# A scheduler that keeps ScalarE's table, with begin times and first clock slices from the trace: a two-layer decoder trunk on one core

## The chip, the core and the metric

The kernel runs on one core of a Trainium2 chip. The metric is device time in microseconds: the median of three runs of the program. The engines are named as in the profile: PE (TensorE, with PEld for its weight loads), ACT (ScalarE), DVE (VectorE), POOL (GpSimd) and SP (SyncE, which here issues every DMA).

## The reference, cut to what matters

Two groups of tokens, 512 of a prompt and 8 x 8 of samples, go through two layers that share their weights. Layer 0 mixes by trailing means (windows 2, 4, 8 and 16) and a 256 x 256 map per group; layer 1 is a gated DeltaNet mixer with 16 value heads; a SwiGLU feed-forward net (FFN) follows each mixer, and RMS norms stand around everything.

```python
for i in range(DEPTH):                      # 2
    h = rms_norm(x, norm_mix_pre[i])
    if i % 2 == 0:
        m, nb = pool_mixer(h, ...)
    else:
        m, nc, ns = gdn_mixer(h, ...)       # projections, conv, gates, chunked delta rule, gate by silu(z), w_out
    x = x + rms_norm(m, norm_mix_post[i])
    h = rms_norm(x, norm_ffn_pre[i])
    x = x + rms_norm(swiglu(h, ffn_w_in[i], ffn_w_out[i]), norm_ffn_post[i])
```

All is float32. The large products are made of three float32r products of split operands (high x high, low x high, high x low).

## The kernel before, in words

Activations lie with channels on the partitions and the 576 tokens on the free axis, cut in two halves (256 + 320 or 288 + 288). Weights stream from HBM as 512 KB blocks: `wraw` is what a DMA brings, `wh` its rounded high part, made on ACT, and `wl` the rest, made on DVE; PE takes `wh` and `wl` as weights and `hH`, `hL` (or `aH`, `aL`; `dH`, `dL` in layer 0) as the other operand.

No engine's order is written by hand. Between `plan.start()` and `plan.finish()` each call is only recorded, by class `Plan`, with the tiles it reads and writes. `finish` then plays the program through a cost table (`cost`, `forward`): at each step the engine that is free first takes an instruction, by rank (the latest start that `backward` found). `take` chooses among those that are ready. A change of ScalarE's function table is priced at 1283 ns (`TURN`), and `HOLD` says by how many ns of rank an engine may pass over the best instruction for one that needs no change of mode. `refined` repeats this with pushed ranks; the pushes are drawn from seeds, and `CHOSEN` lists the seeds to be used, by stretch of the plan.

`forward` also keeps a model of PE's clock. `phases` holds four windows of 3413 ns that are a quarter apart; a window in which PE did less than the share `LOAD` of work makes PE half as fast in the next, and `fast` is the mean over the four (1.0 is full speed, 2.0 half). Where PE would stand idle for more than 300 ns, `idle_until` puts in fillers: products of `ones` with itself into a free PSUM bank, `ps_w`, that no one reads. One planned filler, a 128 x 128 float32 product, shows as two matmuls in the profile. `LEAVE` and `KEEP` limit them.

The names that the later sections use. At the start: `xt` are tiles of 128 prompt tokens; PE turns them (`ps_A<-ident,xt`), ACT sums their squares and makes the root `xst`, DVE takes the reciprocal and makes the normed `xn`, which PE multiplies by the window masks `bf`, `bm`, `bh`; the results go on as `dH`, `dL`. In the mixer of layer 1, `gates()` makes the decays: `misc` on ACT and DVE, the sum over time on PE (`ps_g<-t_le,misc`), a copy `gcr` that goes to HBM (`gc_d`), and a tile `gts` on DVE that uses the buffer of `gcr` again. `project` is the stream of `ps_m` products of the next head group, which fills PE. `gate()` ends a head: PE turns the head's output `vt` into PSUM (`ps_x<-ident,vt`), a DMA then brings `z` into the place of `vt`, and DVE multiplies the two. Ring `x` has one PSUM bank, so the next head's turn waits for that DVE instruction; below, the time from one turn to the next is called a round. There are four head groups of four heads; in the first three `z` comes by that DMA.

Line 478 is the recording layer's replay, so nearly every row has that line, and the fillers have line 474.

Of the kernel before, what the change touches and what calls it, by code (L numbers as in the profile page):

```python
# [57 lines left out]
class Plan:  # L58
# [15 lines left out]
    HOLD = {"PE": 2500.0, "ACT": 0.0}  # L74
    WINDOW, LOAD = 3413.0, 0.38
# [492 lines left out]
    def forward(self, rank, state=None, until=None):  # L568
# [4 lines left out]
        if state is None:  # L573
            todo = n
            left = [len(o[4]) for o in ops]
            free = dict.fromkeys(self.ENGINES, 0.0)
# [5 lines left out]
            phases = [[self.WINDOW * i / 4, 0.0, 2.0, 0, self.WINDOW * (4 - i) / 4] for i in range(4)]  # L582
            fast = 2.0
# [6 lines left out]
        else:  # L590
# [9 lines left out]
            phases = [p[:] for p in phases]  # L600
# [1584 lines left out]
```

## Time and profile before

| | before |
|---|---|
| time, median of 3 runs | 1514.92 us (1513.43 to 1515.28) |
| time of the profiled execution | 1514.92 us |
| its span | 1513.2 us |
| mean granted TensorE clock | 0.995 |
| PE, PEld busy | 1492.4 us (99%), 1445.6 us (96%) |
| DVE busy | 1130.1 us (75%) |
| ACT busy | 852.2 us (56%) |
| POOL busy | 112.1 us (7%) |
| HBM read, written | 165.60 MB, 30.52 MB |

The profiled execution took 1.72 us more than its span from the first to the last instruction, and its time is the median itself. A matmul's end is modelled and overlaps the next one's start, so the share of PE says that PE seldom stood still, not that it ran at its peak; the waits of PE and the places of the fillers tell more.

### The profile page before, as it was taken

Reading aid. Unit: us, or ns where it says so; the run is one execution under the profiler, and the core shown is the slowest. Engines: PE = TensorE matmul, PEld = TensorE weight load, DVE = VectorE, ACT = ScalarE, POOL = GpSimd, SP = SyncE. Lnnn points to the kernel's source line nnn. Section 1 sums busy time; section 2 is a strip of 40 time slices with the busy share of each in tenths; the row PEclk is TensorE's granted clock in tenths of the full one; section 3 lists DMA queues with packets and bytes.
Section 4 is the critical chain, followed back from the end, with each engine's and each line's share of the span. In section 5 each row is a group of like instructions: output and inputs, shape, how many; then the busy total and the mean of one; then the engine's idle time right before and its main releaser. Section 6 shows DMA issues by size and latency. Waiting matters only on the chain.

```text
span 1513.2 us, 30277 instructions
## 1 busy us (share of the span) xinstructions
PE 1492.4 (99%) x11790; PEld 1445.6 (96%) x11790; DVE 1130.1 (75%) x2280; ACT 852.2 (56%) x1839; POOL 112.1 (7%) x246
## 2 busy tenths in 40 slices
PE   8999999999999999999999999999999999999998
PEld 7999999999999899899899899899999999999997
DVE  6994566668789697996898798657796575756856
ACT  7763543435456865865684794645575453434545
POOL 4210000000001010110121110000110000000000
PEclk9999999999999999999999999999999999999999
DMA  7564233233467343434443534657864432324264
GB/s 191 146 184 127 83 88 92 80 102 111 125 181 194 90 126 111 125 99 125 130 113 94 147 113 127 199 157 215 248 193 145 127 97 86 93 81 121 65 163 136
DMA packets 344854, 197.86 MB, mean 131 GB/s; under 512 B 13499, under 2 KB 337692, under 8 KB 344703
## 3 DMA queue, kind: packets, MB, share of 16 engines
q1 hardware_dynamic: 344711, 195.92, 44.9%
q8 instruction: 93, 1.52, 0.4%
q14 instruction: 50, 0.41, 0.1%
HBM read 165.60 MB, written 30.52 MB: 130 GB/s over the span
## 4 chain that ended last, share of the span: by engine, by line
PE 57%; DVE 4%; ACT 2%; DMA 2%; issue 1%; SPq 0%; ACTq 0%; DVEq 0%
PE ps_m L478 16%; PE ps_A L478 15%; PE ps_B L478 14%; PE ps_s L478 5%; PE ps_k L478 4%; PE ps_x L478 2%; DVE vt L478 1%; DVE ac L478 1%; PE ps_n L478 1%; DMA vt<-z_d 1%; DVE wl L478 1%; DVE ii L478 0%; DMA out_dram<-St 0%; ACT wh L478 0%; DMA og<-og_d 0%
## 5 line engine op out<-in xcount | busy, mean ns | idle before, releaser
L478 ACT ACTIVATE wh<-wraw 128x1024 fp32r<-128x1024 f32 (+4 forms) x239 | 233.3, 979 | 202.6 <-PE ps_B L478 87.2
L478 DVE TENSOR_TENSOR wl<-wraw,wh 128x1024 fp32r<-128x1024 f32 (+4 forms) x238 | 266.2, 1123 | 82.8 <-ACT wh L478 48.1
L478 PE MATMUL ps_m<-hH,wh 128*128 128x320 f32 (+1 forms) x832 | 246.9, 311 | 0.3 <-ACT zz L478 0.3
L478 PE MATMUL ps_m<-hL,wh 128*128 128x320 f32 (+1 forms) x832 | 245.6, 307 | 0.0
L478 PE MATMUL ps_m<-hH,wl 128*128 128x320 f32 (+1 forms) x832 | 244.7, 307 | 0.0
L478 PEld LDWEIGHTS ps_m<-hH,wh 128*128 128x128 f32 x832 | 153.7, 189 | 4.3 <-issue 1.5
L478 PEld LDWEIGHTS ps_m<-hH,wl 128*128 128x128 f32 x832 | 154.1, 189 | 2.6 <-issue 1.3
L478 PEld LDWEIGHTS ps_m<-hL,wh 128*128 128x128 f32 x832 | 154.4, 189 | 1.9 <-issue 0.6
L478 PE MATMUL ps_B<-hH,wl 128*128 128x320 f32 (+1 forms) x444 | 128.7, 304 | 0.0
L478 PE MATMUL ps_B<-hL,wh 128*128 128x320 f32 (+1 forms) x444 | 128.4, 303 | 0.0
L478 PE MATMUL ps_B<-hH,wh 128*128 128x320 f32 (+1 forms) x444 | 128.0, 304 | 0.0
L478 PE MATMUL ps_A<-hH,wl 128*128 128x256 f32 (+1 forms) x432 | 118.9, 291 | 0.0
L478 PE MATMUL ps_A<-hH,wh 128*128 128x256 f32 (+1 forms) x432 | 118.8, 290 | 0.0
L478 PE MATMUL ps_A<-hL,wh 128*128 128x256 f32 (+1 forms) x432 | 118.4, 289 | 0.0
L478 PE MATMUL ps_A<-aL,wh 128*128 128x288 f32 (+2 forms) x408 | 113.8, 296 | 0.0
L478 PE MATMUL ps_A<-aH,wl 128*128 128x288 f32 (+2 forms) x408 | 113.4, 296 | 0.0
L478 PE MATMUL ps_A<-aH,wh 128*128 128x288 f32 (+2 forms) x408 | 113.2, 296 | 0.0
L478 PE MATMUL ps_B<-aH,wl 128*128 128x288 f32 x296 | 83.7, 297 | 0.1
L478 PE MATMUL ps_B<-aH,wh 128*128 128x288 f32 x296 | 83.0, 296 | 0.1
L478 PE MATMUL ps_B<-aL,wh 128*128 128x288 f32 x296 | 83.1, 295 | 0.0
L478 PEld LDWEIGHTS ps_B<-hH,wh 128*128 128x128 f32 x444 | 81.8, 188 | 0.3
L478 PEld LDWEIGHTS ps_B<-hH,wl 128*128 128x128 f32 x444 | 81.8, 188 | 0.1
(458 smaller groups left out, 3976.9 us busy)
## 6 DMA issues: line engine op xcount, KB each, us to landing
wraw<-in_ffn_w_in_dram SPq DMA_DIRECT2D x77, 512.0 KB
wraw<-in_gdn_w_in_dram SPq DMA_DIRECT2D x56, 512.0 KB
graw<-in_ffn_w_in_dram SPq DMA_DIRECT2D x33, 512.0 KB
wraw<-in_ffn_w_out_dram SPq DMA_DIRECT2D x32, 448.0 KB
wraw<-in_gdn_w_out_dram SPq DMA_DIRECT2D x24, 512.0 KB
wraw<-in_ffn_w_out_dram SPq DMA_DIRECT2D x32, 320.0 KB
St<-in_state_gdn_rec_dram SPq DMA_DIRECT2D x32, 256.0 KB
out_dram<-St SPq DMA_DIRECT2D x32, 256.0 KB
```

The source lines that it names most:

```text
L478: calls[e](*a, **k)
```

## The change

The diff, without the long table of seeds:

```diff
-    HOLD = {"PE": 2500.0, "ACT": 0.0}
-    WINDOW, LOAD = 3413.0, 0.38
+    HOLD = {"PE": 2500.0, "ACT": 1500.0}
+    WINDOW, LOAD = 3413.0, 0.40
+    BEGIN = {"PE": 0.0, "ACT": 2250.0, "DVE": 2250.0, "POOL": 2200.0, "SP": 150.0}
+    FIRST = 4250.0
...
     CHOSEN = (
-        "0: 7936 55843 86527 33991 97722 31117 8629 9687 47150 83676 16297 15132 53952 77128 31040 66847 59628 "
...
-            free = dict.fromkeys(self.ENGINES, 0.0)
+            free = dict(self.BEGIN)
...
-            phases = [[self.WINDOW * i / 4, 0.0, 2.0, 0, self.WINDOW * (4 - i) / 4] for i in range(4)]
-            fast = 2.0
+            phases = [[0.0, 0.0, 1.0, 0, self.FIRST + self.WINDOW * (1.0 + i / 4)] for i in range(4)]
+            fast = 1.0
```

ACT may now pass over an instruction for up to 1500 ns of rank rather than change its table. The engines' first planned instructions start at `BEGIN` and not all at zero. The modelled clock begins at full speed and stays there until the first windows end, 7663 to 10222 ns after the plan's zero, where before it began at half. `CHOSEN` has 2633 seeds in five strings in place of 2377 in four. No instruction computes anything else: the products are the same, and only the order, the engine of a few instructions that may run on either DVE or POOL, the fillers (31 in place of 21) and the table loads (27 in place of 26) differ. The orders of all engines differ in detail nearly everywhere. The source lines move by 18: 478 is now 496, and 474 is 492.

The first place is PE at the very start: fillers, the turning of the first `xt` tiles, and the first product with `xn`. Before:

```order
L474 MATMUL ps_w<-ones 128x128 x6
L478 MATMUL ps_A<-ident,xt 128x128 x12
L478 MATMUL ps_A<-bf_143,xn 128x128
L478 MATMUL ps_A<-ident,xt 128x128 x4
L478 MATMUL ps_n_169<-ident,prow 128x73
L478 MATMUL ps_A<-bf_143,xn 128x128
```

And now:

```order
L492 MATMUL ps_w<-ones 128x128 x13
L496 MATMUL ps_A<-ident,xt 128x128 x8
L492 MATMUL ps_w<-ones 128x128 x4
L496 MATMUL ps_A<-ident,xt 128x128 x8
L496 MATMUL ps_A<-bf_143,xn 128x128
L492 MATMUL ps_w<-ones 128x128
L496 MATMUL ps_A<-bf_143,xn 128x128
```

Thirteen fillers stand ahead of the first turn of `xt` where six stood, and four more inside the sixteen turns.

The second place is ACT in `gates()`, from the logarithm (`misc`) on; `bet` is the sigmoid, `qks` and `ac` are silus, `gce` is an exponential. Before:

```order
L478 ACT_TABLE_LOAD
L478 ACTIVATE misc<-misc 128x80
L478 ACTIVATE u,ksq<-ps_x 128x128 x3
L478 ACTIVATE u<-ps_m 128x256
L478 ACTIVATE u<-ps_m 128x8x8
L478 ACTIVATE u<-ps_e 128x256
L478 ACTIVATE ac<-u,cwt 128x600
L478 ACT_TABLE_LOAD
L478 ACTIVATE bet<-misc 128x80
L478 ACTIVATE gcr<-ps_g 16x512
```

And now:

```order
L496 ACT_TABLE_LOAD
L496 ACTIVATE misc<-misc 128x80
L496 ACTIVATE ac<-u,cwt 128x600
L496 ACT_TABLE_LOAD
L496 ACTIVATE qks<-ac 128x64
L496 ACTIVATE gcr<-ps_g 16x512
L496 ACTIVATE u<-ps_e 128x256
L496 ACTIVATE wh<-wraw 128x1024
```

One table load stands between the logarithm and `gcr` in both; it was the sigmoid's and is now the silu's, and the sigmoid comes later.

The third place is PE in the second head group, where the first group's heads are turned (`ps_x<-ident,vt`) between products of the projection; shown is the end of the first round, up to the second head's turn. Before:

```order
L478 MATMUL ps_k<-T_1791,Uw 64x32 x32
L478 MATMUL ps_m<-hH,wl 128x320
L478 MATMUL ps_m<-hH,wh 128x320
L478 MATMUL ps_m<-hL,wh 128x320
L478 MATMUL ps_m<-hH,wl 128x320
L478 MATMUL ps_m<-hH,wh 128x320
L478 MATMUL ps_m<-hL,wh 128x320
L478 MATMUL ps_m<-hH,wl 128x320
L478 MATMUL ps_m<-hH,wh 128x320
```

And now the whole round, from the first head's turn to the second's:

```order
L496 MATMUL ps_x<-ident,vt 128x128 x4
L496 MATMUL ps_m<-hH,wl 128x320
L496 MATMUL ps_m<-hH,wh 128x320
L496 MATMUL ps_m<-hL,wh 128x320
L496 MATMUL ps_m<-hH,wl 128x320
L496 MATMUL ps_m<-hH,wh 128x320
L496 MATMUL ps_k<-T_1791,Uw 64x32 x32
L496 MATMUL ps_m<-hL,wh 128x320
L496 MATMUL ps_m<-hH,wl 128x320
L496 MATMUL ps_m<-hH,wh 128x320
L496 MATMUL ps_m<-hL,wh 128x320
L496 MATMUL ps_x<-ident,vt 128x128 x4
```

The first round held eight products of 320 columns and six of 256 (two ahead of the rows shown, four behind them) and now holds nine of 320; the small products `T,Uw` are in both.

309 rows, old and new, of the table CHOSEN are left out of this document.

## The prediction

> **What bounds the kernel now.** I read the page first, then the waits of PE, then the timelines at the places where PE has fillers or waits. The first row is section 1 of the page (busy us, share, count), the second the row of ScalarE's table loads among the groups of instructions (busy us, mean ns, idle before).
>
> ```profile
> PE 1492.4 (99%) x11790; PEld 1445.6 (96%) x11790; DVE 1130.1 (75%) x2280; ACT 852.2 (56%) x1839; POOL 112.1 (7%) x246
> ...
> L478 ACT ACT_TABLE_LOAD x25 | 32.1, 1283 | 2.4 <-DMA misc<-in_gdn_a_log_dram 2.0
> ```
>
> PE is the bound: it counts as busy for 99% of the span, and the other engines have room, ACT 44% of it. So an order can win only what PE loses to waits, fillers and its half clock; it cannot shorten the products. The waits of PE are 17 rows, which add up to 14.2 us; here are the first, two that matter below, and the last (us in total, times, longest):
>
> ```profile
> PE ps_x L478 <- DVE vt L478: 3.4, 5, 1.5
> ...
> PE ps_s L478 <- DVE rv L478: 1.2, 1, 1.2
> ...
> PE ps_x L478 <- DMA crow<-in_state_gdn_conv_dram: 1.2, 1, 1.2
> ...
> PE ps_B L478 <- ACT yT L478: 0.2, 1, 0.2
> ```
>
> Of the 14.2 us, some 4.1 lie in the first 14 us, 3.4 in the turns of finished heads, 1.2 each at the gates and at the conv state, and about 4.3 in small pieces. That is the whole prize, with the half clock at the start and the fillers beside it. The profiled execution took 1514.92 us, 1.72 more than its span, and is the median itself, so I add to 1514.92. A measurement of this kernel tells 0.2%, or 3.0 us, from no change.
>
> **The change part by part.** *ScalarE's table.* The changed program has 27 loads in place of 26. At 1283 ns the added one is 1.3 us of ACT, which is idle 44% of the time: 0 on the path, at most 1.3 where PE waits just there, and no gain, as no load goes. At the gates one load stands between the logarithm and the copy `gcr` as before, only the sigmoid's is now the silu's.
>
> *The start.* PE's timeline (start, us, what, idle before), with fillers on line 474:
>
> ```profile
> 1.27 2.93 PE L474 MATMUL ps_w<-ones 128*128 128x128 f32 x12 [1.27 <-POOL ones L253]
> ...
> 4.42 3.02 PE L478 MATMUL ps_A<-ident,xt 128*128 128x128 f32 x12 [0.23 <-DMA xt<-in_x_prompt_dram]
> ...
> 9.71 0.49 PE L478 MATMUL ps_A<-bf,xn 128*128 128x128 f32 x2 [2.27 <-DVE xn L478]
> ...
> 10.04 0.60 PE L478 MATMUL ps_A<-ident,xt 128*128 128x128 f32 x4
> ...
> 11.59 0.63 PE L478 MATMUL ps_A<-bm,xn 128*128 128x128 f32 x2
> ...
> 13.88 0.58 PE L478 MATMUL ps_A<-dH,wh 128*128 128x256 f32 x1
> ```
>
> The same stretches with their clock (the third number from the end of a row):
>
> ```profile
> 0.00:7.20 7.20, 5.66 (x24) 4.99 (x24) 3.56 (x14) 4.62 (x10) 6.57 (x55) 1.00 0.67 225
> ...
> 10.60:17.50 6.90, 6.61 (x31) 6.26 (x30) 4.72 (x12) 4.85 (x10) 3.58 (x10) 0.51 1.01 285
> ```
>
> The clock's column says 1.00 up to 7.2 us, but PE's rows contradict it: twelve turns take 3.02 us at 4.42 (0.25 each) and four take 0.60 at 10.04 (0.15 each), and at 11.59, in the stretch at 0.51, two products take 0.63. So PE begins at half speed, while the changed plan begins at full speed and puts thirteen fillers ahead of the first turn. Six took 2.93 us, 0.49 each; thirteen take 6.3 and end at 7.6, so the turn starts 3.2 us later than at 4.42. What hides that is in ACT's and DVE's timelines:
>
> ```profile
> 5.55 0.60 ACT L478 ACTIVATE x<-ps_A 128x512 f32<-128x512 f32 x1
> 6.04 0.28 ACT L478 ACTIVATE xst<-xst,epsd 128x1 f32<-128x1 f32 x1
> ...
> 8.57 0.28 DVE L478 RECIPROCAL xst<-xst 128x1 f32<-128x1 f32 x1
> ```
>
> ACT copies the first turned tile at 5.55 and makes the root only behind it, at 6.04, in both orders; DVE, busy with masks, came to the reciprocal at 8.57. With everything 3.2 us later the root ends at 9.5 and the reciprocal follows 0.9 late, and `xn`, `bf` and `dH` with it. Against that, the seventeen fillers among the turns keep PE busy up to `bf`, where it stood idle for 2.27 us. If that keeps the clock full through 10.6 to 17.5, the half stretch is saved; but up to 13.88 PE waits for ACT and DVE anyway, and of the 3.6 us left half is saved, 1.8. I take 1.8 - 0.9 = **-0.9**, between -3.4 (all of 6.9 us at full speed) and +0.9 (the clock as before).
>
> The Trainium skill ("TensorE: Matmul & The Clock Gate", "Part 1: The HAM clock gate") says that half speed is the default state, that a free-running window of 3413 ns of activity releases it, and that one should not fit to a count of slow matmuls, since the phase differs from run to run. The rows of 4.42 and 10.04 agree with the half-speed start; that the phase differs no run here shows. By that rule the start's term would fall anywhere from -3.4 to +0.9, and the sum below between 1512.2 and 1516.5.
>
> *The end of layer 0's FFN.* PE's fillers there, with the next product behind each:
>
> ```profile
> 442.70 0.83 PE L474 MATMUL ps_w<-ones 128*128 128x128 f32 x6
> ...
> 443.68 0.37 PE L478 MATMUL ps_B<-aH,wh 128*128 128x288 f32 x1
> ...
> 457.66 0.38 PE L474 MATMUL ps_w<-ones 128*128 128x128 f32 x2
> ...
> 458.22 0.39 PE L478 MATMUL ps_e<-hH,wl 128*128 128x256 f32 x1 [0.18 <-DVE wl L478]
> ```
>
> Three fillers and the gap behind them cost 0.98 us, one costs 0.56. Before there are two groups of three and one of one, 2.5 us; now three of one, 1.7: **-0.8**, between -2.5 (none needed) and +0.8 (the waits are there and the filler only covers less).
>
> *The turns.* Each head's turn needs the bank that the one before frees, through the reload of `z` and a DVE product:
>
> ```profile
> 700.01 0.66 PE L478 MATMUL ps_x<-ident,vt 128*128 128x128 f32 x4 [0.24 <-ACT nco L478]
> 700.83 2.06 PE L478 MATMUL ps_k<-T,Uw 128*64 128x32 f32 x64
> 702.82 0.42 PE L478 MATMUL ps_m<-hH,wl 128*128 128x320 f32 x1
> 704.80 0.63 PE L478 MATMUL ps_x<-ident,vt 128*128 128x128 f32 x4
> 710.98 0.66 PE L478 MATMUL ps_x<-ident,vt 128*128 128x128 f32 x4 [1.54 <-DVE vt L478]
> ...
> 819.22 0.60 PE L478 MATMUL ps_x<-ident,vt 128*128 128x128 f32 x4
> 825.57 0.66 PE L478 MATMUL ps_x<-ident,vt 128*128 128x128 f32 x4 [0.68 <-DVE vt L478]
> 830.83 0.66 PE L478 MATMUL ps_x<-ident,vt 128*128 128x128 f32 x4 [0.26 <-DVE vt L478]
> ```
>
> The rounds are 4.79 us (no wait), 6.18 (of it 1.54 waited), 6.35 (0.68) and 5.26 (0.26): a mean of 5.65. From 702.82 to 704.80 eight products of 320 columns and four of 256 took 1.98 us, 0.18 and 0.14 each, a turn about 0.4, and the 64 small matmuls of `T,Uw` 2.0 (700.83 to 702.82). By these prices the changed order has this much work of PE from turn to turn: in the first group 9 x 0.18 + 2.0 + 0.4 = 4.0, then ten of 256 and three of 320 with 64 small ones, 4.3, then 4.2; in the second 7.1, 5.1 and 5.3. At the mean round the waits are 1.65 + 1.35 + 1.45 + 0 + 0.55 + 0.35 = 5.4; I keep 0.5 for the other groups. Before it was 3.4: **+2.5**. At rounds of 4.75 the waits are 1.75 + 0.5 and the term -1.2; at 6.35 they are 8.9 + 0.5 and it is +6.0.
>
> *The gates.* PE's timeline, then `gcr` on ACT, its store on SP, and `gts` on DVE:
>
> ```profile
> 521.86 0.38 PE L478 MATMUL ps_g<-t_le,misc 128*16 128x128 f32 x2
> 522.17 1.05 PE L478 MATMUL ps_x<-ones,sqs 128*128 128x1 f32 x8
> 523.15 0.83 PE L478 MATMUL ps_g<-t_le,misc 128*16 128x128 f32 x6
> 527.68 0.61 PE L474 MATMUL ps_w<-ones 128*128 128x128 f32 x4
> 529.51 0.36 PE L478 MATMUL ps_s<-gts,s_gt_r 128*128 128x256 f32 x1 [1.22 <-DVE rv L478]
> ...
> 524.77 0.57 ACT L478 ACTIVATE gcr<-ps_g 16x512 f32<-16x512 f32 x1
> ...
> 525.37 0.33 SPq L478 DMA_DIRECT2D gc_d<-gcr  x1
> ...
> 528.94 0.42 DVE L478 TENSOR_TENSOR gts<-s_in,gHL 128x256 fp32r<-128x256 f32 x1 [1.30 <-DMA gc_d<-gcr]
> ```
>
> `gts` waits for the store, since it takes the buffer of `gcr`; from `t_le` (521.86) to the product with `gts` (529.51) 7.65 us pass, of which 1.83 (from 527.68) are two fillers and a wait. The changed order puts between them ten more products of 320 columns (1.8), two of 256 (0.3), four turns (0.6), and only one of the four `ones,sqs` (-0.7 of 0.98): 5.82 + 2.0 = 7.8 us of work, against a chain of 7.65 - 0.7 = 6.9. The wait is covered and one filler of 0.56 stays: **-1.3**, between -1.8 and 0, if the chain starts later.
>
> *The rest.* In the third group two fillers are new, between 0.56 and 0.98: **+0.8** (0 to 1.0). The conv state's third load is moved behind two weight loads on SP's queue, but PE's two turns of it stand as close as before: 0, between -1.2 and +1.0. At the tail two fillers go:
>
> ```profile
> 1501.33 0.39 PE L474 MATMUL ps_w<-ones 128*128 128x128 f32 x2
> ...
> 1502.01 0.44 PE L478 MATMUL ps_B<-ident,nh 128*128 128x128 f32 x2 [0.30 <-DVE xa L478]
> ```
>
> From filler to next turn 0.68 us, twice; but the waits for `xa` and `nh` that they covered stay in part: **-0.5**, between -1.4 and 0. The small waits of 4.3 us are dealt anew by any new order: 0, between -4 and +4.
>
> The sum: -0.9 - 0.8 + 2.5 - 1.3 + 0.8 - 0.5 = -0.2, or 1514.92 - 0.2 = **1514.7**.
>
> **The rivals.** *Slower by long rounds.* PE has less work between the first group's turns than before, and the bank stays the only one. With every round at 6.35, as from 819.22 to 825.57, the term is +6.0 in place of +2.5: 1514.7 + 3.5 = 1518.2. It decides from a mean round of 6.3 on. For it: three of four rounds seen are over 5.2. Against it: those that waited are seen because they were long, and the one that was covered shows at most 4.79.
>
> *Faster by short rounds.* With the reload as in the first round the term is -1.2: 1514.7 - 3.7 = 1511.0. For it: 700.01 to 704.80. Against it: three longer ones.
>
> *The change does not do what it says.* The loads do not get fewer, and the clock's first slices are read as full where PE's rows say half: the fillers delay the start, the clock stays half up to 17.5, and the start costs 0.9 in place of -0.9: 1516.5. With the delay passed on in full (3.2) it is 1518.8. The Trainium skill's rule of the free-running window (the page and section above) would make this rival a matter of the run.
>
> **How the numbers follow.** The sum as it stands (1512 to 1517.9): 0.35. Long rounds, or small waits that add as much: 0.28. Short rounds, or small waits that go: 0.30. The start that costs: 0.07, of which 0.04 within 0.2% and 0.03 above. So faster by over 0.2% (below 1511.9) 0.30, the same 0.39, slower (above 1517.9) 0.31. The range that leaves out 2 in 10: from 1511.0 the other bounds (start, small waits) reach down to 1509.5, from 1518.2 up to 1520.5. Alone, the likeliest case holds 1512 to 1517.9.
>
> **What would show it.** Start: the first turn of `xt` near 7.6 us, the reciprocal near 9.5, and the stretch from 10.6 to 17.5 at a clock near 1.00; a first turn near 4.9 would mean that PE began at full speed. Gates: no wait of PE at the product with `gts`. Turns: PE's wait for `vt` at 5 to 6 us in all, most of it in the first group. FFN end: three single fillers with gaps of 0.5 us. The prediction is wrong if PE's waits add up to less than 11 or more than 18 us, or if the products themselves take another time between waits.

## The result, and the profile after

The changed kernel takes 1516.77 us (median of 20 runs, 1514.43 to 1518.9), the kernel before 1513.65 us in the same comparison (20 runs, 1510.63 to 1515.95). The ratio is 1.0019, 95% interval 1.0012 to 1.0025: slower by some 2.9 us, where no change was forecast. The profiled execution of the changed kernel took 1517.07 us, with a span of 1515.3. Section 1 of its page, and its table loads among the groups of instructions (27 loads, of which one stands apart by its operands):

```profile
PE 1495.9 (99%) x11810; PEld 1446.9 (95%) x11810; DVE 1131.2 (75%) x2279; ACT 852.1 (56%) x1840; POOL 108.3 (7%) x247
...
L496 ACT ACT_TABLE_LOAD x26 | 33.4, 1283 | 2.6 <-DMA misc<-in_gdn_a_log_dram 2.2
```

PE is busy for 3.5 us more than before (1492.4), with 20 more rows, the ten more fillers. The waits of PE after, in 21 rows:

```profile
PE ps_k L496 <- DVE QD L496: 1.5, 3, 0.8
PE ps_w L492 <- POOL ones L271: 1.3, 1, 1.3
PE ps_B L496 <- ACT nh L496: 1.3, 4, 0.5
PE ps_x L496 <- DVE vt L496: 0.9, 2, 0.6
PE ps_m L496 <- ACT hH L496: 0.8, 2, 0.4
...
PE ps_B L496 <- DVE wl L496: 0.6, 2, 0.4
PE ps_A L496 <- ACT wh L496: 0.6, 2, 0.4
PE ps_A L496 <- DVE wl L496: 0.5, 2, 0.3
```

The wait for `vt` is 0.9 us (3.4 before), those for `rv` and `crow` (1.2 each) are gone, and all 21 rows together come to 11.4 us, 2.8 less than before. Yet the kernel is slower: waits do not tell the story. So I compared stages. PE's products are the same ones in both programs, and at many places both orders have done exactly the same products; the time at such a place can be compared. The table has, from PE's rows in the traces of both kernels and of the spliced ones (the first five experiments, the ninth and the eleventh), how long each stage took wherever its order was the one before and wherever it was the changed one, so that most stages have several executions of each:

```
stage, ends at (us)        before: profile  all, median (n)      changed: profile  all, median (n)      changed - before
start                27         27.07       26.46 (4)              24.81       25.18 (5)               -1.3
                    125         97.76       97.86 (6)             100.04       99.25 (2)               +1.4
FFN, layer 0        430        305.20      305.23 (5)             304.90      304.90 (3)               -0.3
its end             470         39.98       39.98 (5)              39.19       39.22 (4)               -0.8
                    487         17.11       17.10 (6)              17.59       17.59 (3)               +0.5
conv state, gates   549         61.93       59.87 (6)              61.01       60.86 (3)               +1.0
                    660        110.69      110.42 (6)             111.24      111.24 (3)               +0.8
turns of groups 1,2 824        164.27      163.94 (6)             162.49      162.95 (3)               -1.0
                   1000        175.94      175.41 (7)             177.00      177.68 (2)               +2.3
last group, output 1072         72.09       72.10 (7)              73.40       73.19 (2)               +1.1
FFN, layer 1       1207        134.85      134.92 (6)             136.15      135.32 (3)               +0.4
                   1480        272.99      273.03 (6)             272.69      272.69 (3)               -0.3
tail                end         33.34       33.34 (6)              34.84       34.11 (3)               +0.8
```

The differences of these medians sum to +4.5 us, against some 3 measured. No single stage has it all: the changed order wins 3.7 us in five stages and loses 8.2 in eight, 3.4 of them from 824 to 1072 us. In the FFNs, the last group and the tail the executions of the order before agree within 0.5 us. The exception that matters is the stage of the gates in the order before: 59.4 to 59.9 us in four executions, and 61.9 and 62.9 us in two, one of which is the profile from which I predicted.

The clock does not explain the loss. The mean granted clock over the changed kernel's 20 runs is 0.9968, and over 33 runs of the kernel before, beside the first four experiments, 0.9958. Of the runs at 0.998, six of the changed kernel took 1515.1 to 1517.7 us and six of the kernel before 1512.5 to 1515.0.

### The profile page after: what moved, and what is told of

The parts are those of the page before. It is cut to its first block, busy times and chain, and to the rows that moved or that the text cites. A ratio compares the mean times of both kernels' runs of the same rounds, so it can differ in the third digit from the quotient of the medians.

```text
span 1515.3 us, 30329 instructions
## 1 busy us (share of the span) xinstructions
PE 1495.9 (99%) x11810; PEld 1446.9 (95%) x11810; DVE 1131.2 (75%) x2279; ACT 852.1 (56%) x1840; POOL 108.3 (7%) x247
## 4 chain that ended last, share of the span: by engine, by line
PE 84%; DVE 5%; ACT 4%; DMA 4%; issue 2%; POOL 1%; SPq 0%; DVEq 0%; ACTq 0%; POOLq 0%
PE ps_A L496 26%; PE ps_B L496 26%; PE ps_m L496 18%; PE ps_s L496 5%; PE ps_k L496 4%; PE ps_x L496 2%; DVE wl L496 2%; DMA wraw<-in_ffn_w_in_dram 1%; PE ps_e L496 1%; ACT wh L496 1%; PE ps_n L496 1%; DMA og<-og_d 1%; DMA vt<-z_d 0%; DVE nacc L496 0%; DMA wraw<-in_ffn_w_out_dram 0%
```

## The experiments

Twelve kernels were run. Most are splices: a program plans both orders and issues the one up to PE's operation with a given number, then what is left in the other's order.

**Which stage does it.** The only edit is the order issued (`old` is planned with the settings and seeds before, `new` with the changed ones; the number is where PE leaves a list):

```diff
-            for i, e in best[1]:
+            for i, e in self.spliced((new, 752), (old, None)):                  # first
+            for i, e in self.spliced((old, 752), (new, 5713), (old, None)):     # second
+            for i, e in self.spliced((old, 5713), (new, 7481), (old, None)):    # third
+            for i, e in self.spliced((old, 7481), (new, None)):                 # fourth
```

> The changed order up to PE's operation 752 (125.4 us in both traces), and the order before from there on. In the two traces the changed kernel is 2.0 us ahead at 50 us and level at 125. Theory of places (what a stage loses or gains in the trace belongs to its order): equal to the kernel before, within 0.5 us, with a half-clock stretch again near 49 to 52 us and waits of PE for wl near 83 and for wh near 122. Rival, accident (the half clock and the two late weights at 49 to 122 us are of that one execution): 1.5 to 2 us faster than before.

Measured: 1511.91 us, ratio 0.9992 (0.9983 to 1.0001). Between the two theories: 1.2 us faster, with an interval from 2.6 us faster to level. The half-clock stretch came again, at 49.0 us, and so did a wait for `wl`.

> The order before up to operation 752 and from 5713 on (125 and 824 us), the changed order between: the end of layer 0's FFN, the gates and the first two groups of heads. The changed kernel's lead grows there from 0.0 to 2.7 us. Theory of places: 2.7 us faster than before (ratio 0.9982), faster than both kernels. Rival, debt (the lead is work that is only dealt to later, to be paid behind the cut): within 0.7 us of before.

Measured: 1515.20 us, ratio 1.0013 (1.0004 to 1.0022), so slower by 2, a miss for both. Three things speak to it. The lead of 2.7 us was measured against a profile whose gates were 2.1 us late by accident (the table); by the medians these stages come to +0.2. The mean granted clock over its eleven runs is 0.9950, against 0.9958 for the kernel before beside it, by an estimate from these figures 1.2 us of 1514. And in the profiled execution PE ran at half clock just behind the splice, as the windows show (us, PE busy, then the other engines, with the granted clock third from the end). What is left of the 2.0 stays open.

```profile
826.00:829.30 3.30, 1.94 (x60) 1.83 (x58) 2.11 (x3) 2.28 (x4) 1.16 (x2) 1.00 0.02 5
829.30:836.10 6.80, 6.80 (x79) 6.13 (x79) 1.53 (x4) 2.75 (x8) 0.00 (x0) 0.50 0.59 157
```

> The changed order only from operation 5713 to 7481 (824 to 1072 us: the last groups of heads and the second output projection), the order before around it. In the traces the lead shrinks there from 2.7 to 0.4 us. Theory of places: 2.3 us slower than before (ratio 1.0015). Rival, debt (the loss is the other side of the lead of the stage ahead, and goes with it): within 0.7 us of before.

Measured: 1517.07 us, ratio 1.0021 (1.0012 to 1.0030): slower by 3.2, the theory of places. This one stage alone makes a kernel as slow as the whole change. PE's time over these stages, by equal products, first in the kernel before and in the fourth, which has the same order there, then in the changed kernel and in this one (us, then PE busy):

```profile
824.00:1072.03 248.03, 245.59 (x2171) 231.21 (x2170) 185.00 (x409) 152.99 (x414) 16.01 (x32) 1.00 0.56 165
```
```profile
820.14:1067.64 247.50, 245.56 (x2171) 231.18 (x2170) 184.97 (x409) 152.95 (x414) 15.64 (x32) 1.00 0.57 165
```
```profile
821.27:1071.66 250.39, 248.46 (x2171) 232.33 (x2170) 185.28 (x409) 153.53 (x414) 17.88 (x36) 1.00 0.56 162
```
```profile
824.53:1075.87 251.34, 248.47 (x2171) 232.10 (x2170) 186.03 (x409) 153.10 (x414) 18.09 (x33) 1.00 0.55 162
```

PE stands idle for 2.4 and 1.9 us in the order before and for 1.9 and 2.9 us in the changed one, so the waits do not tell the two apart. The same products, between the waits and at full clock, do: they keep PE busy for 245.4 to 245.7 us in the seven executions of the order before that ran these stages at full clock, and for 248.5 us in this kernel and in the changed one (248.9 and 248.7 in the eighth and the twelfth kernel, which have the same order of PE there). These 2.9 us are the size of the loss.

A part of them can be placed. From about 1000 to 1020 us, without any wait, the same products take 21.37 us in this kernel and in the changed one (equal to 0.01), and 20.22 in the fourth. PE's timeline there, first this kernel, then the fourth:

```profile
1008.56 0.63 PE L635 MATMUL ps_k<-St,kx 128*32 128x256 f32 x4
...
1013.39 1.92 PE L635 MATMUL ps_k<-St,kx 128*32 128x256 f32 x28
```
```profile
1004.87 1.93 PE L635 MATMUL ps_k<-St,kx 128*32 128x256 f32 x32
```

The 32 small products of `St,kx` run as 4 and 28 instead of together, 2.55 us for 1.93; products of the projection (`ps_m`) and other small ones stand between. Over all of 824 to 1072 us there are 128 of them, in four rows of 32 before and in rows of 32, 32, 2, 30, 4 and 28 now. Counted from each start to PE's next start, without waits, they take 8.54 us in the changed order and 7.46 in the fourth kernel: 1.1 of the 2.9, half of it at each split. The rest is spread over many kinds of small products, some of which got cheaper. That the splitting is the cause is read from these rows; no run undoes one split alone.

> The order before up to operation 7481 (1072 us), the changed order from there: layer 1's FFN and the tail. In the traces the changed kernel loses 1.4 us there up to PE's last product and 1.1 more behind it, with waits of PE for wl and wh near 1114, 1146, 1179 and 1487 us. Theory of places: 2 to 2.5 us slower than before, with these waits again. Rival, accident (the weights came late in that one execution): within 0.7 us of before, without them.

Measured: 1514.64 us, ratio 1.0008 (0.9999 to 1.0017), slower by 1.2 (from level to 2.6). Between the two theories, and of the waits for weights only one of 0.2 us came again: of the 1.3 us that the changed profile loses from 1072 to 1207 us, 0.9 was of that execution (the table). The tail's came again (7.7 to 7.8 us from the start of PE's last product to the end in all four executions of the changed tail, 6.6 in all of the one before). The stores of SP, before and after:

```profile
1508.30 1.12 SPq L478 DMA_DIRECT2D out_dram<-xb  x2
```
```profile
1508.59 1.12 SPq L496 DMA_DIRECT2D out_dram<-xb  x2
1509.80 0.53 SPq L496 DMA_DIRECT2D out_dram<-xa  x1
```

In the changed order a store of `xa` is still to be issued behind the two of `xb`.

The four pieces sum to +5.2 us, each known to within 1.4, so they agree with the 2.9 of the whole only within the noise.

**The splice of what each does better.**

```diff
+            for i, e in self.spliced((new, 65), (old, 1821), (new, 3312), (old, None)):   # fifth
```

> The changed order up to PE's operation 65 (21.9 us before) and from 1821 to 3312 (259 to 470 us: layer 0's FFN with its end), the order before elsewhere. In the traces so far the changed order's first 27 us take 24.8 us, against 25.7 to 27.2 in four executions of the order before, its FFN from 259 to 470 us 0.3 to 0.6 less, and its other stages as much or more. Theory of places: 1.5 to 2.5 us faster than before (ratio 0.9985), faster than both kernels. Rival, debt (a stage's lead is paid behind its end): within 0.7 us of before.

Measured: 1510.83 us, ratio 0.9983 (0.9974 to 0.9992): 2.6 us faster than before (1.2 to 3.9) and so faster than both kernels, close to the 1.5 to 2.5 of the theory of places.

> The changed order only up to PE's operation 65 (21.9 us before), the order before from there: the changed start alone. In the traces so far the stage to 27 us took 24.7 to 25.2 us in five executions of the changed start and 27.4 in a sixth, and 25.7 to 27.2 in four of the start before. Theory that the lead lasts: 1.1 us faster than before (ratio 0.9993; the prediction's term was 0.9). Rival, the weights' ring takes it back (what PE gains it waits for in layer 0's FFN, whose loads come no earlier): within 0.4 us of before, with the lead gone by 430 us.

Measured, with `spliced((new, 65), (old, None))`: 1510.84 us, ratio 0.9987 (0.9979 to 0.9996). The changed start alone makes a kernel 1.9 us faster (0.6 to 3.2). The interval holds the 1.1 of the first theory and leaves out the rival's 0.4, but the rival has a part in it: in the profiled execution the lead over the profile before is 1.9 us up to 100 us, then 0.8 at 125, where PE waits 0.6 us for `nsq`, and 0.4 at 430. What the start gives goes with the clock: over this kernel's eleven runs the mean granted clock is 0.9976, over the fifteen of the kernel before beside them 0.9959. Most of the fifth kernel's gain is then the start's; whether layer 0's FFN adds to it, these two intervals cannot tell.

> The changed order, with operations 5713 to 7481 (824 to 1072 us) in the order before: the reverse of the third experiment. Theory of places: the changed kernel's loss of 3 us goes with that stage alone, so 1513.5 to 1514.5, level with before; the waits of PE for hH near 950 us and the split St,kx near 1010 us are gone, and what the changed order wins at the start and at layer 0's FFN still pays for its late weights in layer 1's FFN. Rival, many small causes with none that decides: 1515.5 or more.

Measured, with `spliced((new, 5713), (old, 7481), (new, None))`: 1514.54 us, ratio to before 1.0008 (0.9998 to 1.0017). With the late stage put back, some 1.7 of the 2.9 us go; the two intervals overlap, and by its ratio the kernel lies between the two theories. As expected the waits for `hH` and the split are gone, and the products from 824 to 1072 us take 245.4 us again. Its start, though the changed one, took 27.4 us: here the clock came late.

**Late weights.** The changed kernel's chain of waits runs through the ring of weights: `wl` is made, its raw buffer becomes free, the next weight is loaded, `wh` is made of it, and PE waits for that:

```profile
112.38 2.35 DVE wl L496 x2
114.74 0.03 DVE aL L496
114.77 6.57 DMA wraw<-in_ffn_w_in_dram
...
121.36 1.07 ACT wh L496
...
122.47 0.56 PE ps_B L496 x2
```

Two kernels put the making and loading of weights ahead (`early` moves an operation ahead of others on its own engine, never past a source):

```diff
-        return best[1]
+        return self.early(new, ("wh_", "wl_", "wraw_"), 2)    # sixth: 375 operations, up to 2 places
+        return self.early(new, ("wl_",), 1)                   # twelfth: wl in the FFNs, 1 place
```

> The changed order, with every load of a weight and every making of its halves wh and wl put ahead of up to two operations that stand before it on its engine, where none of them is its own source. PE's order is the same. PE's waits for wl and wh in the changed kernel's trace (83, 122, 446, 954, 1114, 1146, 1179 and 1487 us) cost 0.35 to 0.55 us each, some 3.4 in all. Theory of late weights: 1.5 to 3 us faster than the changed kernel, near the kernel before. Rival, displaced (what they are put ahead of comes late in their stead): within 0.7 us of the changed kernel, with new waits of PE for hH, aH or xn.

Measured: 1695.84 us, ratio 1.1196 (1.1172 to 1.1221).

> The changed order, with each making of wl on VectorE in the two FFNs put ahead of one operation that stands before it there, where that is not its source: 152 of them move by one place; loads, wh and PE's order stay. The changed kernel's chain of waits runs wl, load of the next weight (5.8 to 6.6 us), wh, PE near 114, 1136 and 1479 us. Theory of the ring (a late wl makes the next load late): PE's waits for wl and wh in the FFNs fall by half, and the kernel is 1 to 2 us faster than the changed one. Rival, displaced (what is put behind comes late in its stead, or VectorE stands at a wl whose wh isn't made): as fast as the changed kernel or slower.

Measured: 1606.11 us, ratio 1.0632 (1.0612 to 1.0652). The sixth is far outside either theory. In the twelfth the rival came, though some 90 us slower than the changed kernel was not thought of. The first two rows are waits of VectorE in the changed kernel and in the twelfth, the last two waits of SP's queue in the changed kernel and in the sixth:

```profile
DVE wl L496 <- ACT wh L496: 59.0, 47, 7.4
```
```profile
DVE wl L635 <- ACT wh L635: 116.3, 101, 7.3
```
```profile
SPq L496 <- DVE wl L496: 391.1, 111, 14.7
```
```profile
SPq L635 <- DVE wl L635: 500.6, 100, 15.4
```

In the twelfth VectorE stood at a `wl` whose `wh` was not made 101 times, against 47, and what is behind comes late. PE has waits there that the changed kernel has not, of which this is the largest:

```profile
PE ps_n L635 <- DVE nacc L635: 9.5, 8, 2.1
```

The Trainium skill ("TensorE: Matmul & The Clock Gate", "Architectural detail: the array is 16× 32×32, not 1× 128×128") calls ScalarE and VectorE strict first-in first-out queues; the 101 waits agree with it. So that late weights cost the changed kernel its waits is read from the chain, not shown by an experiment; these two show how little room the order has.

**The settings and the search.**

```diff
-    HOLD = {"PE": 2500.0, "ACT": 0.0}
+    HOLD = {"PE": 2500.0, "ACT": 1500.0}      # all else, and the seeds, as before
```

> The planner before in everything, its list of seeds too, but ScalarE's hold at 1500 in place of 0. The seeds were found for the hold of 0. Theory of the search (the time is the list's, and the list fits only its own settings): slower by over 1%, since the order has 126 fillers in place of 21, and 28 table loads in place of 26. Rival, the setting itself gains: at most 0.3% slower.

Measured: 1573.19 us, ratio 1.0394 (1.0381 to 1.0408). The theory of the search came: a constant changed under a list of seeds that was found for another value costs 4%. So the change cannot be split into its constants and its list: the time is that of the one order that they make together.

**Fillers.**

```diff
+        return [(i, e) for i, e in new if e is not None]      # eighth; the tenth does so behind operation 1000 of the fifth
```

> The changed order without any of its 31 fillers (62 matmuls). Theory of the clock (the fillers hold the clock at full speed): slower than the changed kernel by 2 us or more, with half-clock stretches behind the places of the fillers, and a slow start as in the kernel before. Rival, the fillers cost more than they give: 1 to 3 us faster than the changed kernel, since the 18 behind the start cost 0.3 to 0.5 us each where PE would have less to wait.

Measured: 1520.76 us (1512.92 to 1533.17), ratio to before 1.0042 (1.0022 to 1.0062), slower than the changed kernel by 3.5 us or so, with four times the spread. The clock of the profiled execution (1529 us), by windows:

```profile
29.00:32.40 3.40, 2.82 (x19) 2.44 (x18) 3.00 (x7) 1.88 (x7) 0.00 (x0) 1.00 0.23 52
32.40:66.50 34.10, 34.10 (x140) 31.94 (x139) 19.84 (x52) 17.22 (x45) 4.57 (x6) 0.50 0.21 64
```

Without its fillers PE falls to half clock there for 34 us, so the theory of the clock holds for the start; the mean granted clock of the twelve runs lies between 0.983 and 0.997. Where the changed kernel has its others, nothing is lost: the end of layer 0's FFN takes 39.19 us in both. And the two runs in which the clock stayed up (0.996 and 0.997) took 1513.0 and 1512.9 us, less than any of the changed kernel's 20, so at a full clock the fillers do seem to cost something, as the rival said.

> The spliced order of the fifth experiment, without the seven fillers that stand behind PE's operation 1000 (the end of layer 0's FFN, the gates and the tail). Theory of cover (such a filler stands where PE would wait as long anyway): within 0.7 us of the fifth experiment. Rival, a filler's own length delays what follows: 0.5 us at each of four places, 2 us faster. Rival of the clock: a half-clock stretch behind one of the places, 1.7 us slower or more in some executions.

Measured: 1512.16 us, ratio 0.9993 (0.9984 to 1.0002), against 0.9983 for the fifth kernel; the intervals overlap, so nothing is settled but that two microseconds are not to be had. One half-clock stretch, 707.4 to 710.8 us, stands in its profile, behind a window with a turn's wait in which PE was busy for 1.76 of 3.40 us.

## Why the prediction was wrong

The step that failed is the one under the whole sum: an order can win only what PE loses to waits, fillers and its half clock, since it cannot shorten the products. The sum takes it that an order cannot lengthen them either: for what the new order does outside the named places it has 0, and thinks of waits alone. The runs showed the products themselves: from 824 to 1072 us the same products keep PE busy for 248.5 us in the changed order and for 245.4 to 245.7 before. These 2.9 us are the size of the whole loss.

That the time came out 2.1 us from the forecast 1514.7 is luck. Large errors cancel: by the table the turns, with the third group's fillers, came out 4.3 us better than their terms, the gates 2.3 worse, the tail 1.3 worse, and the stages without a term 5.9 worse. And the base of 1514.92 stands 1.3 us above the median of 20 runs. Part by part:

**The start (-0.9).** Right in sign, too small. The stage to 27 us is 1.3 us shorter by the medians, and the changed start alone made a kernel 1.9 us faster (0.6 to 3.2). PE's timeline after:

```profile
1.27 4.66 PE L492 MATMUL ps_w<-ones 128*128 128x128 f32 x26 [1.27 <-POOL ones L271]
6.03 1.07 PE L496 MATMUL ps_A<-ident,xt 128*128 128x128 f32 x8
...
8.70 0.40 PE L496 MATMUL ps_A<-bf,xn 128*128 128x128 f32 x2
...
12.44 0.39 PE L496 MATMUL ps_A<-dH,wh 128*128 128x256 f32 x1
```

The first turn comes at 6.03 us, not at 7.6, because the clock rose to full at 4.42 amid the fillers; the reciprocal comes at 7.51 and not near 9.5, and the stretch from 10.6 to 17.5 is at full clock as forecast. In the ninth kernel the same fillers took 5.91 us and the first turn came at 7.28:

```profile
1.27 5.91 PE L631 MATMUL ps_w<-ones 128*128 128x128 f32 x26 [1.27 <-POOL ones L420]
7.28 0.96 PE L635 MATMUL ps_A<-ident,xt 128*128 128x128 f32 x7
```

So the price swings with the execution: with the order before, the first stretch at full clock began at 4.18, 6.51, 7.24 and 13.53 us in four executions. The Trainium skill ("TensorE: Matmul & The Clock Gate", "Part 1: The HAM clock gate") says of its free-running window that the phase differs from run to run; these four agree. The rival of a start that costs did not come by the medians; in the ninth kernel's profiled execution, with 27.4 us up to 27, it did (25.7 to 27.2 in the four before).

What the start wins the changed order loses again up to 125 us (+1.4): a half-clock stretch in some executions and two late weights, neither in the sum.

```profile
45.40:48.80 3.40, 3.40 (x24) 2.81 (x23) 3.10 (x8) 2.08 (x6) 0.34 (x1) 1.00 0.86 288
48.80:52.20 3.40, 3.40 (x14) 3.40 (x14) 2.96 (x9) 1.67 (x5) 2.15 (x3) 0.50 0.54 158
```

In the ninth kernel, with the same order there, the same work stayed at full clock:

```profile
48.00:51.40 3.40, 3.40 (x24) 2.81 (x23) 3.10 (x8) 2.09 (x6) 0.33 (x1) 1.00 0.87 290
51.40:54.80 3.40, 3.40 (x27) 3.40 (x27) 3.40 (x11) 3.00 (x10) 2.16 (x3) 1.00 0.55 158
```

**The end of layer 0's FFN (-0.8).** Right in the number: three single fillers, and -0.8 us in the stage. But it is not the fillers that cost: with none of them the stage takes 39.19 us (eighth kernel) and 39.21 (tenth), as with three. They stand where PE waits anyway, and the changed order waits less there (1.9 us with the fillers, 2.5 before). One of the gaps is 0.77 us and not 0.56, since PE waits for `wl` behind it, and the next stage loses 0.5:

```profile
445.54 0.38 PE L492 MATMUL ps_w<-ones 128*128 128x128 f32 x2
446.31 0.40 PE L496 MATMUL ps_B<-aH,wl 128*128 128x288 f32 x1 [0.39 <-DVE wl L496]
```

**The turns (+2.5).** Wrong in sign: waits for `vt` of 0.9 us in all (3.4 before), and the stage to 824 us 1.0 shorter. The turns after:

```profile
700.33 0.60 PE L496 MATMUL ps_x<-ident,vt 128*128 128x128 f32 x4
704.73 0.66 PE L496 MATMUL ps_x<-ident,vt 128*128 128x128 f32 x4 [0.29 <-DVE vt L496]
709.84 0.44 PE L496 MATMUL ps_x<-ident,vt 128*128 128x128 f32 x2 [0.58 <-DVE vt L496]
...
715.84 0.60 PE L496 MATMUL ps_x<-ident,vt 128*128 128x128 f32 x4
```

Rounds of 4.40, 5.11 and 6.00 us, of which 0.29, 0.58 and 0 waited: PE had 4.1, 4.5 and 6.0 us of work between the turns where I counted 4.0, 4.3 and 4.2, and the chain through the reload took 4.4 and 5.1 where it was waited for, not the mean of 5.65. The step that failed in this term is to take the mean of four rounds for the length of a chain: a round that PE fills with other work is as long as that work. Only rounds in which PE waited bound the chain, and it varied from 4.4 up. In two of these rounds DVE itself stands idle until the reload of `z` has landed:

```profile
703.92 0.75 DVE L496 SCALAR_TENSOR_TENSOR vt<-ps_x,prm,vt 128x512 f32<-128x512 f32 x1 [2.10 <-DMA vt<-z_d]
...
709.03 0.75 DVE L496 SCALAR_TENSOR_TENSOR vt<-ps_x,prm,vt 128x512 f32<-128x512 f32 x1 [3.63 <-DMA vt<-z_d]
```

So these rounds end with the reload, while in the round of 6.35 us before it was DVE itself that was busy, with a transposition of `ii` (1.16 us), right up to its product at 824.77. The rival of long rounds falls with it: the kernel came to its side, by other means.

**The gates (-1.3).** No wait at `gts`, and one filler left, as forecast; and yet +1.0 us in the stage. The waits that I priced come in some executions only. The fourth kernel, with the order before there, and the conv state's turn in it:

```profile
525.30 0.60 PE L631 MATMUL ps_w<-ones 128*128 128x128 f32 x4
525.97 0.39 PE L635 MATMUL ps_s<-gts,s_gt_r 128*128 128x256 f32 x1
```
```profile
494.61 0.42 PE L635 MATMUL ps_x<-ident,crow 24*128 24x24 f32 x4
```

No wait at either. The 1.2 for `rv` is in none of the other five traces of that order, and a wait for `crow` in two of them (1.4 us in the third kernel, 0.4 in the eleventh). In the changed order, on the other hand, PE waits in this stage for `zz`, `glp`, `QD` or `vt`, 0.6 to 1.1 us in all three traces. I priced the removal of something that was mostly not there, and so the changed kernel seemed to gain 0.9 us in that stage, where it loses 1.0 against the median of the order before.

**The third group's fillers (+0.8)** are there and take 1.0 us with the gap behind them, in a stage that is shorter in all. **The tail (-0.5)** is +0.8: on PE the forecast came, 0.5 us less up to its last product in two of three executions (the third has a new wait of 0.4 for `wh`), but behind that product, where the stores are and I did not look, 1.2 us were added. **The small waits (0)** hold the step that decides: new waits for `hH`, `QD`, `wl` and `wh` stand in several of the eight stages that lose, but the largest loss, from 824 to 1072 us, is of the products. Elsewhere the products differ by less, from some 0.6 us more (gates) to some 0.5 less (turns). By the table, the stages that no other term covers (27 to 430, 470 to 487, 549 to 660, 824 to 1480 us) come to 1.4 - 0.3 + 0.5 + 0.8 + 2.3 + 1.1 + 0.4 - 0.3 = +5.9 us, a part of it the half-clock stretch near 50 us, where I had 0 with ±4 beside it. Of the signs of an error that I named, the waits stayed inside (11.4 us, between 11 and 18), and the other came: the products themselves took another time between the waits.

## What to carry to other kernels

When PE is 99% busy and an order is replaced, compare stages by equal work done, not waits, and split the difference into idle and busy time: here the listed waits fell by 2.8 us and the kernel grew by 2.9, because products that are the same took longer in another order. Take a second execution of the kernel before if there is one; a wait that stands in one trace may belong to that execution, and a gain must not be booked for it. And a list of tuned orders fits only its own settings: splicing the better stages of two lists (0.9983, most of it from the start) was worth more than either list, and one constant changed under a list cost 4%.

## What was not expected of the hardware

A window of 3.4 us can be followed by a half-clock window in the midst of the kernel, and not only where PE stood: behind windows in which PE was busy for 1.94 of 3.30 and 1.76 of 3.40 us, and also behind one that shows it busy for all of 3.40 (45.4 to 48.8 us, with 24 rows, many of them products of few rows and columns). Where the half clock falls depends on the execution: in the first experiment, with the same order there, it came at the same place (49.0 us; full clock had begun at 4.64 us, in the changed kernel at 4.42), and in the ninth, where full clock had begun at 7.32, the same work stayed at full clock. Which work counts for the gate stays open.

The time of the same matmuls depends on their order: at full clock and between waits, the same 2171 matmuls took 245.4 to 245.7 us in seven executions of one order and 248.5 in two of another. Two rows of 32 small products that the second order splits take 0.5 us more each.

The order on VectorE has no slack here: 152 of its operations moved by one place each, with every dependence kept, cost 90 us.
